# Compressed branch of a sparse attention kernel: four heads' probabilities turned by one transpose into a diagonal of blocks, values held four times

## The chip, the cores and the metric

One core of one Trainium2 chip runs the whole program. The metric is the device time of one execution in microseconds (us), the median of the runs shown. Engines are called as in the profile: PE (TensorE matmul), PEld (TensorE weight load, which overlaps PE), DVE (VectorE), ACT (ScalarE), POOL (GpSimd), SP (SyncE, which issues the DMAs).

## The reference, cut to what matters

The program is one transformer layer on 512 tokens of width 1024, all in float32: a gated feed-forward block, a mixer with two attention groups, a second feed-forward block, a last norm. One attention group (eight query heads in two key groups of four, head size 64) has three branches: a compressed one (31 block summaries as keys and values), a selected one and a windowed one, added with gates. The change touches the compressed branch alone:

```python
kc = compress_blocks(kc_raw, ...)        # 31 compressed keys per key group
vc = compress_blocks(vc_raw, ...)        # 31 compressed values per key group
s = jnp.einsum('btgrd,bcgd->bgrtc', q, kc) * ATTN_SCALE
s = jnp.where(mask_c, s - slopes[:, :, None, None] * dist_c, NEG_INF)
p_cmp = jnp.where(mask_c, jax.nn.softmax(s, axis=-1), 0.0)
o_cmp = jnp.einsum('bgrtc,bcgd->btgrd', p_cmp, vc)
...
return g[..., 0:1] * o_cmp + g[..., 1:2] * o_slc + g[..., 2:3] * o_win
```

With 8 selection blocks and 16 to choose, the selected branch is ordinary causal attention. For each block of 128 queries and each key group, `p_cmp` is four heads of 128 x 32 (the 32nd column is padding).

## The kernel before, in words

Every float32 matmul operand is split into a high part (float32r, a cast on ACT) and a low part (the difference, a subtraction on DVE), and a product takes two or three matmuls of these parts.

The order of the program is: the first feed-forward block, the mixer, the second feed-forward block. In the mixer, eight stages of the sliding-window group (class `Swa`) come first and then the stages of the sparse group (class `Nsa`): for key groups g = 0, 1 and query blocks i = 0 to 3, one stage with br = 0 for i = 0 and two stages, br = 1 (selected) and br = 2 (windowed), for i > 0. The compressed branch is computed within br = 0 and br = 2, so eight times in all.

A stage has two halves. `scores` (L1042 to L1133) makes the scores of four heads on PE (lines 985, 986, and a bias matmul on 1062, 1065, 1077 or 1098) in PSUM tiles `sc`, of which there are three. DVE takes the maximum (L1058, L1078), ACT the exponential (L1059, L1084), then DVE (L1116, L1117, L1128) and for one head in four ACT (L1126) scale the probabilities. The compressed probabilities of the four heads lie beside one another in one tile `small` (128 queries x 4 heads x 32), scaled on L1132. `outputs` (L1135 to L1153) makes a list of blocks and hands it to `times_values` (L1016): for each block `transposed` (L991) turns the probabilities of four heads by four PE transposes (L994) into one PSUM tile `mm`, ACT casts them into the high part (L996), DVE takes the low part (L997), and two matmuls (L1031 with the high part, L1032 with the low part) add values times probabilities into one PSUM tile `pv` (64 rows of the values' high part, 64 of their low part). The transposes of a block are written ahead of the matmuls of the block before. After the last block `put_o` (L1000) takes `pv` out: ACT copies the low rows (L1002), DVE adds them (L1007, twice), ACT and DVE split the sum (L1013, L1014). There is only one buffer for `pv`, so the first L1031 of the next stage waits for L1007.

In the compressed block the four transposes have 32 columns of probabilities as their weights and the identity as moving operand; the results, 32 x 128 each, lie side by side in rows 0 to 31 of `mm`. L996 and L997 work on 32 x 512 and write rows 0 to 31 of a fixed tile `ct` (the profile calls it `u` like others), whose other rows were set to zero at the start, as those of the values' tile `CV` were (L809). So the two matmuls of this block multiply 128 rows of which 96 are zero. `CV` gets its values on L895 and L896, once, before the first stage that needs them.

While the stages run, projections and the output product of the mixer (L216 to L218, three matmuls a step) are put in between as filler work by `attend`, by shares written as numbers. The order of instructions on each engine is then set when the program is built, by a scheduler with its own estimates of durations; a small change can move many instructions. On the chip each engine takes its queue in that order.

Of the kernel before, what the change touches and what calls it, by code (L numbers as in the profile page):

```python
# [12 lines left out]
AF = mybir.ActivationFunctionType  # L13
ALU = mybir.AluOpType
AX = mybir.AxisListType

P = 128
# [29 lines left out]
def tile_hybrid(ctx, tc, xT, f1_wi, f1_wo, wm_t, wm_n, cw1, cw2, small, wm_oa, wm_ob, wm_oc, f2_wi, f2_wo, const, out):  # L47
    nc = tc.nc
    V, A, PE = nc.vector, nc.scalar, nc.tensor
# [4 lines left out]
    def f(ap):  # L54
        return ap.bitcast(F32)

    def ps(tag="mm"):
        return psp.tile([P, 512], F32, tag=tag, name=tag, bufs=NB[tag])
# [8 lines left out]
    def flat(dt=F32R):  # L67
        return sb.tile([P, 1024], dt, tag="u", name="u", bufs=NU)

    def unit(dt=F32R):  # L70
        return flat(dt).rearrange("p (a t) -> p a t", a=2)
# [4 lines left out]
    def tmp():  # L76
        return sb.tile([P, 512], F32, tag="tmp", name="tmp", bufs=NTMP)
# [16 lines left out]
    ident = sb.tile([P, P], F32, tag="ident", name="ident")  # L94
# [708 lines left out]

    CV = sb.tile([P, 2, 2, HD], F32R, tag="cv", name="cv")
    ct = unit()
    zero = ones.unsqueeze(1).to_broadcast([P, 4, P])
    A.activation(CV.rearrange("p g a d -> p (g a d)").rearrange("p (a t) -> p a t", t=P), zero[:, :2], AF.Copy, scale=0.0)  # L809
    for a in range(2):  # L810
        A.activation(ct[:, a, :].rearrange("p (a t) -> p a t", t=P), zero, AF.Copy, scale=0.0)

# [57 lines left out]
    def network_o(kv):  # L870
        hT, w2 = state["hT", kv]
        po = ps()
        if kv == 0:
            for c in range(2):
                PE.matmul(po[:HD, :62], w2[:, c, :], hT[:, c, :], start=c == 0, stop=c == 1)
            kc = tmp()
            V.memset(kc[:HD, :64], 0.0)
            V.tensor_copy(
                kc[:HD, :64].rearrange("p (g c) -> p g c", g=2)[:, :, :NCMP],
                po[:HD, :62].rearrange("p (g c) -> p g c", g=2),  # L880
            )
            for g in range(2):
                put_key(kc[:HD, g * 32 : g * 32 + 32], 0, KT[g][0][:, 512:544], KT[g][1][:, 512:544])
        else:
            vc = tmp()
            V.memset(vc[:32, :128], 0.0)
            for g in range(2):
                for c in range(2):
                    PE.matmul(
                        po[:NCMP, g * HD : (g + 1) * HD], hT[:, c, g * NCMP : (g + 1) * NCMP], w2[:, c, :],  # L890
                        start=c == 0, stop=c == 1,
                    )
            V.tensor_copy(vc[:NCMP, :128], po[:NCMP, :128])
            vcv = vc[:32, :128].rearrange("p (g d) -> p g d", g=2)
            A.copy(CV[:32, :, 0, :], vcv)  # L895
            V.tensor_tensor(CV[:32, :, 1, :], vcv, f(CV[:32, :, 0, :]), op=ALU.subtract)  # L896
        yield 0.6


# [4 lines left out]
    def put_key(src, g, k1, k2):  # L904

        own = slice(g * HD, (g + 1) * HD)
        oth = slice((1 - g) * HD, (2 - g) * HD)
        A.copy(k1[own], src)
        V.tensor_tensor(k2[own], src, f(k1[own]), op=ALU.subtract)
        nc.sync.dma_start(f(k1[oth]), f(k1[own]))  # L910
        nc.sync.dma_start(f(k2[oth]), f(k2[own]))

    def keys(b, kind):
        o = ps()
        yield from proj(b, o)
        if kind == "b":
            SK.extend([unit(), unit()])
        elif not KT:
            for _ in range(2):
                k12 = double(F32R)  # L920
                KT.append([k12[:, :1056], k12[:, 1056:]])
        kz = tmp()
        V.tensor_tensor(kz, o, state["bc"], op=ALU.mult)
        for g in range(2):
            rows = slice(g * HD, (g + 1) * HD)
            if kind == "b":
                put_key(kz[rows, :], g, SK[0][:, g, :], SK[1][:, g, :])
            else:
                c = 544 if kind == "w" else 0
                put_key(kz[rows, :], g, KT[g][0][:, c : c + 512], KT[g][1][:, c : c + 512])  # L930


    VT = []
# [54 lines left out]
    def small_t(n, name):  # L988
        return sb.tile([P, n], F32, tag="st" + name, name=name, bufs=3)

    def transposed(pl, rows, cols):  # L991
        pt = ps()
        for r in range(4):
            PE.transpose(pt[:rows, r * P : (r + 1) * P], pl[r][:, cols], ident)  # L994
        u = unit() if rows == P else ct
        A.copy(u[:rows, 0, :], pt[:rows, :])  # L996
        V.tensor_tensor(u[:rows, 1, :], pt[:rows, :], f(u[:rows, 0, :]), op=ALU.subtract)  # L997
        return u

    def put_o(pv, kb0, i):  # L1000
        low = tmp()
        A.copy(low[lo, :], pv[hi, :])  # L1002
        pvv = pv.rearrange("p (a two t) -> p a two t", a=2, two=2)
        lov = low.rearrange("p (a two t) -> p a two t", a=2, two=2)
        ob = tmp()[:, :256].rearrange("p (a t) -> p a t", a=2)
        for par in range(2):
            V.tensor_tensor(ob[par * HD : (par + 1) * HD], pvv[lo, :, par, :], lov[lo, :, par, :], op=ALU.add)  # L1007
        ts = slice(i * P, (i + 1) * P)
        for a in range(2):
            if OB[kb0 + a] is None:  # L1010
                OB[kb0 + a] = unit()
            u = OB[kb0 + a]
            A.copy(u[:, 0, ts], ob[:, a, :])  # L1013
            V.tensor_tensor(u[:, 1, ts], ob[:, a, :], f(u[:, 0, ts]), op=ALU.subtract)  # L1014

    def times_values(work, pv, first, last):  # L1016

        ahead = None
        for n in range(len(work) + 1):
            if n < len(work):  # L1020
                pl, cols, rows, v = work[n]
                cur = transposed(pl, rows, cols), rows, v
                if n == 0:
                    yield 0.44
            else:
                cur = None
            if ahead is not None:
                u, rows, v = ahead
                a = first and n == 1
                b = last and n == len(work)  # L1030
                PE.matmul(pv, v, u[:, 0, :], start=a, stop=False)  # L1031
                PE.matmul(pv, v, u[:, 1, :], start=False, stop=b)  # L1032
                yield 0.87 if n < len(work) else 0.43
            ahead = cur

    class Nsa:
# [98 lines left out]
        def outputs(self):  # L1135
            g, i, br = self.g, self.i, self.br
            if br != 2:
                state["pv"] = ps("pv")
            pv = state["pv"]

            def values_of(b, kb):
                return VT[b][:, kb, g].rearrange("p a d -> p (a d)")

            if br == 0:
                work = [(self.p, slice(b * P, (b + 1) * P), P, values_of(b, 0)) for b in range(2)]
            else:
                work = [(self.p, slice(kb * P, (kb + 1) * P), P, values_of(br - 1, kb)) for kb in range(i + 1)]
            if br != 1:
                cl = [self.c[:, r, :] for r in range(4)]
                work.append((cl, slice(0, 32), 32, CV[:, g].rearrange("p a d -> p (a d)")))  # L1150
            yield from times_values(work, pv, br != 2, br != 1)
            if br != 1:
                put_o(pv, g * 2, i)  # L1153

    class Swa:
# [41 lines left out]
        def outputs(self):  # L1197
            g, i, W, c0 = self.g, self.i, self.W, self.c0
            pv = ps("pv")
            work = [  # L1200
                (self.p, slice(n * P, (n + 1) * P), P, VT[2][:, c0 // P + n, g].rearrange("p a d -> p (a d)"))
                for n in range(W // P)
            ]
            yield from times_values(work, pv, True, True)
            put_o(pv, 4 + g * 2, i)
# [68 lines left out]
    kb, vals = keys(8, "b"), values()  # L1274
# [15 lines left out]
    piece("c1", compressed(1))  # L1290
    piece("kw", keys(3, "w"))
    piece("o0", network_o(0))
    piece("n1", network(1))
    piece("q4", queries(4))
    piece("q5", queries(5))
    piece("o1", network_o(1))
    piece("q6", queries(6))
    piece("q7", queries(7))
# [122 lines left out]
```

## Time and profile before

| | before |
|---|---|
| median of 3 runs | 972.81 us (972.71 to 972.96) |
| the profiled execution | 972.98 us, of which the span shown is 971.2 us |
| granted clock of TensorE | 0.998 |
| PE busy | 957.0 us (99% of the span) |
| DVE busy | 814.8 us (84%) |
| ACT busy | 633.0 us (65%) |

The profile is of one execution. Matmuls are pipelined, and the busy time of PE includes the end of each one under the start of the next, so 99% does not mean that no time is lost on PE. The distance between the starts of two matmuls is what one costs when PE is the bound. "Idle before" names the engine whose semaphore came last.

### The profile page before, as it was taken

Reading aid. Unit: us, or ns where it says so; the run is one execution under the profiler, and the core shown is the slowest. Engines: PE = TensorE matmul, PEld = TensorE weight load, DVE = VectorE, ACT = ScalarE, POOL = GpSimd, SP = SyncE. Lnnn points to the kernel's source line nnn. Section 1 sums busy time; section 2 is a strip of 40 time slices with the busy share of each in tenths; the row PEclk is TensorE's granted clock in tenths of the full one; section 3 lists DMA queues with packets and bytes.
Section 4 is the critical chain, followed back from the end, with each engine's and each line's share of the span. In section 5 each row is a group of like instructions: output and inputs, shape, how many; then the busy total and the mean of one; then the engine's idle time right before and its main releaser. Section 6 shows DMA issues by size and latency. Waiting matters only on the chain.

```text
span 971.2 us, 13622 instructions
## 1 busy us (share of the span) xinstructions
PE 957.0 (99%) x5008; PEld 809.6 (83%) x5008; DVE 814.8 (84%) x1442; ACT 633.0 (65%) x1273; POOL 3.2 (0%) x7
## 2 busy tenths in 40 slices
PE   9999999999999999999999999999999999999996
PEld 7888888888888889788777888888888888888886
DVE  6999889888798675788899899999987988879864
ACT  8786666575766545554777776768667666676654
POOL 0000000000000000000000000000000000000000
PEclk9999999999999999999999999999999999999999
DMA  8233414234125213123310112223331423312122
GB/s 318 63 130 122 142 44 141 80 116 142 44 76 184 100 45 109 44 80 103 131 44 16 73 44 71 93 77 114 124 141 44 140 77 120 136 48 95 49 64 86
DMA packets 36387, 93.98 MB, mean 97 GB/s; under 512 B 4449, under 2 KB 8929, under 8 KB 36321
## 3 DMA queue, kind: packets, MB, share of 16 engines
q1 hardware_dynamic: 35648, 92.82, 27.7%
q8 instruction: 39, 0.64, 0.3%
q10 hardware_dynamic: 672, 0.30, 0.1%
q14 instruction: 28, 0.22, 0.1%
HBM read 89.40 MB, written 2.10 MB: 94 GB/s over the span
## 4 chain that ended last, share of the span: by engine, by line
PE 90%; DVE 4%; ACT 4%; issue 1%; DMA 1%; SPq 0%; POOL 0%; DVEq 0%; ACTq 0%
PE mm L352 18%; PE mm L353 9%; PE sc L352 7%; PE mm L218 4%; PE mm L216 4%; PE mm L217 4%; PE sc L353 4%; PE pv L441 4%; PE pv L443 3%; PE sc L441 3%; PE sc L442 3%; PE pv L442 3%; PE sc L443 3%; PE mm L994 2%; PE pv L1031 2%; PE sc L985 1%
## 5 line engine op out<-in xcount | busy, mean ns | idle before, releaser
L352 PE MATMUL mm<-u 128*128 128x512 f32 x760 | 273.6, 396 | 0.2 <-ACT mm L625 0.2
L353 PE MATMUL mm<-u 128*128 128x256 f32 x760 | 211.2, 279 | 0.0
L352 PEld LDWEIGHTS mm<-u 128*128 128x128 f32 x760 | 142.5, 188 | 34.2 <-DVE tmp L643 0.8
L353 PEld LDWEIGHTS mm<-u 128*128 128x128 f32 x760 | 143.2, 188 | 6.1
L352 PE MATMUL sc<-u 128*128 128x512 f32 x304 | 110.7, 396 | 0.0
L216 PE MATMUL mm<-u 128*128 128x512 f32 x220 | 88.3, 402 | 0.0
L217 PE MATMUL mm<-u 128*128 128x512 f32 x220 | 86.7, 394 | 0.0
L218 PE MATMUL mm<-u 128*128 128x512 f32 x220 | 86.5, 393 | 0.0
L353 PE MATMUL sc<-u 128*128 128x256 f32 x304 | 84.9, 279 | 0.0
L352 PEld LDWEIGHTS sc<-u 128*128 128x128 f32 x304 | 57.1, 188 | 13.2
L405 DVE TENSOR_TENSOR u<-tmp,u 128x512 fp32r<-128x512 f32 (+1 forms) x96 | 60.6, 641 | 8.0 <-ACT u L404 8.0
L404 ACT CAST u<-tmp 128x512 fp32r<-128x512 f32 (+1 forms) x96 | 54.8, 585 | 18.6 <-PE sc L443 13.6
L617 ACT COPY tmp<-mm 128x256 f32<-128x256 f32 x76 | 28.4, 374 | 50.5 <-PE mm L353 50.5
L353 PEld LDWEIGHTS sc<-u 128*128 128x128 f32 x304 | 57.2, 188 | 3.0
L441 PE MATMUL pv<-u 128*128 128x512 f32 x144 | 57.3, 398 | 0.0
L441 PE MATMUL sc<-u 128*128 128x512 f32 x144 | 57.1, 397 | 0.0
L443 PE MATMUL pv<-u 128*128 128x512 f32 x144 | 56.9, 395 | 0.0
L442 PE MATMUL sc<-u 128*128 128x512 f32 x144 | 56.7, 394 | 0.0
L442 PE MATMUL pv<-u 128*128 128x512 f32 x144 | 56.6, 393 | 0.0
L443 PE MATMUL sc<-u 128*128 128x512 f32 x144 | 56.2, 390 | 0.0
L330 DVE TENSOR_TENSOR u<-t,u 128x1024 fp32r<-128x1024 f32 x38 | 46.5, 1222 | 4.9 <-ACT u L327 2.8
L218 PEld LDWEIGHTS mm<-u 128*128 128x128 f32 x220 | 41.3, 188 | 8.2
(266 smaller groups left out, 2267.1 us busy)
## 6 DMA issues: line engine op xcount, KB each, us to landing
t<-in_f_wi_dram SPq DMA_DIRECT2D x87, 512.0 KB, 4.4
tmp<-in_f_wo_dram SPq DMA_DIRECT2D x80, 256.0 KB, 4.7
t<-in_wm_t_dram SPq DMA_DIRECT2D x13, 512.0 KB, 4.0
t<-in_cw_dram SPq DMA_DIRECT2D x8, 512.0 KB, 4.4
h<-in_xT_dram SPq DMA_DIRECT2D x4, 512.0 KB, 6.9
tmp<-in_f_wo_dram SPq DMA_DIRECT2D x16, 128.0 KB, 4.4
t<-in_wm_oa_dram SPq DMA_DIRECT2D x4, 512.0 KB, 3.9
t<-in_wm_n_dram SPq DMA_DIRECT2D x4, 408.0 KB, 5.2
```

Source lines behind the costliest of these rows:

```text
L216: PE.matmul(o, wh[:, c], xs[k][:, 0, :], start=s0, stop=False)
L217: PE.matmul(o, wh[:, c], xs[k][:, 1, :], start=False, stop=False)
L218: PE.matmul(o, wl[:, c], xs[k][:, 0, :], start=False, stop=s1)
L330: V.tensor_tensor(wl, t[:, 0:1024], f(wh), op=ALU.subtract)
L352: PE.matmul(o, w[0][:, c], x[k], start=new, stop=False, skip_group_check=not first)
L353: PE.matmul(o[:, :256], w[1][:, c], x[k][:, 0], start=False, stop=k == 3, skip_group_check=not first)
L404: A.copy(u[:, 0, :n], raw[:, :n])
L405: V.tensor_tensor(u[:, 1, :n], raw[:, :n], f(u[:, 0, :n]), op=ALU.subtract)
L441: PE.matmul(o, wh[:, c], u[:, 0, :], start=False, stop=False, skip_group_check=True)
L442: PE.matmul(o, wh[:, c], u[:, 1, :], start=False, stop=False, skip_group_check=True)
L443: PE.matmul(o, wl[:, c], u[:, 0, :], start=False, stop=q == j1 - j0 - 1, skip_group_check=True)
L617: A.copy(z, o[:, t2])
```

## The change: what it does

The compressed probabilities of the four heads, 128 x (4 x 32), are turned by one PE transpose of 128 columns (new line 997) in place of four of 32. The result has head r in rows 32r to 32r+31, over the 128 queries. To multiply each head with the same values and still get the four heads side by side in 512 columns, the 128 x 512 tile `ct` takes head r in rows 32r to 32r+31 and columns 128r to 128r+127, a diagonal of blocks; all else in it stays zero from the start. That takes four casts on ACT (new line 1000, 32 x 128 each) in place of one of 32 x 512, and four subtractions on DVE (new line 1002) in place of one. The values `CV` are written to all four quarters of its rows: three more copies on ACT, once (new line 898). The zeroing of `CV` (L809) goes, since all its rows are now written. The two matmuls of the block keep their shapes. The argument `rows` disappears from the list of blocks.

```diff
-    A.activation(CV.rearrange("p g a d -> p (g a d)").rearrange("p (a t) -> p a t", t=P), zero[:, :2], AF.Copy, scale=0.0)
...
             A.copy(CV[:32, :, 0, :], vcv)
             V.tensor_tensor(CV[:32, :, 1, :], vcv, f(CV[:32, :, 0, :]), op=ALU.subtract)
+            for r in range(1, 4):
+                A.copy(CV[r * 32 : r * 32 + 32], f(CV[:32]))
...
-    def transposed(pl, rows, cols):
+    def transposed(pl, cols):
         pt = ps()
+        if cols is None:
+
+            PE.transpose(pt[:, :P], pl.rearrange("p r c -> p (r c)"), ident)
+            at = [(slice(r * 32, r * 32 + 32), slice(r * P, (r + 1) * P)) for r in range(4)]
+            for rows, c in at:
+                A.copy(ct[rows, 0, c], pt[rows, :P])
+            for rows, c in at:
+                V.tensor_tensor(ct[rows, 1, c], pt[rows, :P], f(ct[rows, 0, c]), op=ALU.subtract)
+            return ct
         for r in range(4):
-            PE.transpose(pt[:rows, r * P : (r + 1) * P], pl[r][:, cols], ident)
-        u = unit() if rows == P else ct
-        A.copy(u[:rows, 0, :], pt[:rows, :])
-        V.tensor_tensor(u[:rows, 1, :], pt[:rows, :], f(u[:rows, 0, :]), op=ALU.subtract)
+            PE.transpose(pt[:, r * P : (r + 1) * P], pl[r][:, cols], ident)
+        u = unit()
+        A.copy(u[:, 0, :], pt)
+        V.tensor_tensor(u[:, 1, :], pt, f(u[:, 0, :]), op=ALU.subtract)
         return u
...
             if br != 1:
-                cl = [self.c[:, r, :] for r in range(4)]
-                work.append((cl, slice(0, 32), 32, CV[:, g].rearrange("p a d -> p (a d)")))
+                work.append((self.c, None, CV[:, g].rearrange("p a d -> p (a d)")))
```

Since the scheduler orders the queues anew, the change also moves other instructions of the sparse stages. Lines behind the added ones have other numbers after the change: 985 and 986 become 987 and 988, the transposes of L994 line 1005, L996 and L997 lines 1007 and 1008, L1002 and L1007 lines 1013 and 1018, L1031 and L1032 lines 1042 and 1043, L1058 and L1059 lines 1069 and 1070, L1062 and L1065 lines 1073 and 1076, L1116, L1117, L1126 and L1128 lines 1127, 1128, 1137 and 1139.

On PE, the end of the second stage with a compressed block (g = 0, i = 1, br = 2), from the low-part matmul of its compressed block to the next stage's work. Before:

```order
L1031 MATMUL pv<-u,cv 128x512
L1032 MATMUL pv<-u,cv 128x512
L985 MATMUL sc<-t_3949,u 128x416
L986 MATMUL sc<-t_3949,u 128x416
L1065 MATMUL sc<-u 128x32
L1062 MATMUL sc<-u 128x384
L217 MATMUL mm<-u 128x512
L218 MATMUL mm<-u 128x512
L994 MATMUL mm<-ident,tmp 128x128 x12
L985 MATMUL sc<-t_3949,u 128x416
L986 MATMUL sc<-t_3949,u 128x416
```

After the change:

```order
L1005 MATMUL mm<-ident,tmp 128x128 x7
L1043 MATMUL pv<-u,cv 128x512
L1005 MATMUL mm<-ident,tmp 128x128 x5
L1042 MATMUL pv<-u 128x512
L1043 MATMUL pv<-u 128x512
L1042 MATMUL pv<-u 128x512
L216 MATMUL mm<-u 128x512
```

The low-part matmul of the compressed block now stands within the next stage's twelve transposes, and only five of them lie between it and the first matmul into the next stage's `pv`.

On DVE, the same place: the subtractions of the compressed block and what follows them. Before:

```order
L997 TENSOR_TENSOR u<-mm,u 32x512
L1116 TENSOR_TENSOR su<-su,ge 128x4
L1058 TENSOR_REDUCE nm<-sc 128x1
L1117 RECIPROCAL su<-su 128x4
L1058 TENSOR_REDUCE nm<-sc 128x1
L1128 TENSOR_SCALAR tmp<-tmp,su 128x384 x3
L1007 TENSOR_TENSOR tmp<-pv,tmp 64x256 x2
```

After the change:

```order
L1002 TENSOR_TENSOR u<-mm,u 32x128
L1127 TENSOR_TENSOR su<-su,ge 128x4
L1002 TENSOR_TENSOR u<-mm,u 32x128
L1128 RECIPROCAL su<-su 128x4
L1002 TENSOR_TENSOR u<-mm,u 32x128
L1139 TENSOR_SCALAR tmp<-tmp,su 128x384 x3
L1002 TENSOR_TENSOR u<-mm,u 32x128
L1069 TENSOR_REDUCE nm<-sc 128x1 x3
L1018 TENSOR_TENSOR tmp<-pv,tmp 64x256 x2
```

The last of the four subtractions now stands behind the scaling of the next stage's probabilities, and three reductions stand between it and the two additions that release `pv`.

## Rows read from the trace of the kernel before

**Rows 1.** The page: the span and the busy time of each engine.

```profile
span 971.2 us, 13622 instructions
PE 957.0 (99%) x5008; PEld 809.6 (83%) x5008; DVE 814.8 (84%) x1442; ACT 633.0 (65%) x1273; POOL 3.2 (0%) x7
```

**Rows 2.** Busy time in 476 to 602 us: length, PE, PEld, DVE, ACT, POOL (instructions); granted clock, DMA.

```profile
476.00:602.00 126.00, 123.69 (x677) 101.05 (x676) 115.32 (x289) 98.10 (x296) 0.00 (x0) 1.00 0.15 53
```

**Rows 3.** The chain of waits, 476 to 602 us: shares by line, pieces.

```profile
by line: PE mm L994 14.3%; PE pv L1031 9.9%; PE mm L218 9.7%; PE mm L216 9.7%; PE sc L985 9.6%; PE mm L217 9.6%; PE pv L1032 8.8%; PE sc L986 8.0%; PE sc L1062 6.2%; ACT tmp L1059 2.0%; ACT u L996 1.9%; DVE u L997 1.5%; ACT tmp L1002 1.0%; 
478.34 0.87 PE mm L994 x8
560.67 1.20 PE mm L994 x11
```

**Rows 4.** Groups of instructions, 476 to 602 us, shapes apart: busy us, mean ns, idle before.

```profile
L994 PE MATMUL mm<-ident,tmp 128*128 128x128 f32 x168 | 26.1, 274 | 0.4 <-ACT tmp L1126 0.2 <-DVE tmp L1128 0.2
L994 PE MATMUL mm<-ident,small 128*32 128x128 f32 x32 | 5.1, 272 | 0.0
L996 ACT CAST u<-mm 32x512 fp32r<-32x512 f32 x8 | 4.5, 565 | 0.0
L997 DVE TENSOR_TENSOR u<-mm,u 32x512 fp32r<-32x512 f32 x8 | 5.4, 669 | 0.0
L1014 DVE TENSOR_TENSOR u<-tmp,u 128x128 fp32r<-128x128 f32 x16 | 4.0, 286 | 0.2
L1013 ACT CAST u<-tmp 128x128 fp32r<-128x128 f32 x16 | 4.0, 298 | 1.9 <-DVE tmp L1007 1.9
L1058 DVE TENSOR_REDUCE nm<-sc 128x1 f32<-128x384 f32 x16 | 8.5, 544 | 0.2 <-PE sc L1062 0.2
L1058 DVE TENSOR_REDUCE nm<-sc 128x1 f32<-128x32 f32 x32 | 6.0, 187 | 3.0 <-ACT tmp L1084 1.0 <-ACT tmp L1059 0.9 <-PE sc L1065 0.7
```

**Rows 5.** Single lines: counts, durations in ns min/median/max, first and last start, forms.

```profile
L617 ACT COPY tmp<-mm x76: 357/375/391, 54.8 to 935.4; 128x256 f32<-128x256 f32 x76
L896 DVE TENSOR_TENSOR cv<-tmp,cv x1: 280/280/280, 477.7 to 477.7; 32x128 fp32r<-32x128 f32 x1
L895 ACT CAST cv<-tmp x1: 298/298/298, 476.9 to 476.9; 32x128 fp32r<-32x128 f32 x1
L809 ACT ACTIVATE cv<-ones x1: 399/399/399, 2.6 to 2.6; 128x256 fp32r<-128x256 f32 x1
```

**Rows 6.** Timeline 505 to 509 us, a stage's end: start, duration, engine, line, operation.

```profile
505.17 0.39 PE L1031 MATMUL pv<-u,cv 128*128 128x512 f32 x1
505.40 0.39 PE L1032 MATMUL pv<-u,cv 128*128 128x512 f32 x1
505.83 0.58 ACT L1002 COPY tmp<-pv 64x512 f32<-64x512 f32 x1 [1.49 <-PE pv L1032]
506.72 0.84 DVE L1007 TENSOR_TENSOR tmp<-pv,tmp 64x256 f32<-64x256 f32 x2
508.08 0.49 ACT L1013 CAST u<-tmp 128x128 fp32r<-128x128 f32 x2
508.40 0.49 DVE L1014 TENSOR_TENSOR u<-tmp,u 128x128 fp32r<-128x128 f32 x2
508.90 0.46 PE L985 MATMUL sc<-t,u 128*128 128x416 f32 x1 [0.69 <-ACT small L1059]
```

**Rows 7.** Timeline 490 us: the first use of the compressed values.

```profile
490.20 0.39 PE L1031 MATMUL pv<-u,cv 128*128 128x512 f32 x1
```

**Rows 8.** Timeline at the start: ACT's first work behind L809.

```profile
5.40 0.72 ACT L170 ACTIVATE u<-h,sm 128x512 fp32r<-128x512 f32 x1 [2.43 <-DMA sm<-in_small_dram]
```

**Rows 9.** Waits of PE and of its weight load, 476 to 602 us: total us, times, longest.

```profile
PE sc L985 <- ACT small L1059: 1.0, 2, 0.7
PE sc L985 <- ACT tmp L1059: 0.7, 1, 0.7
PEld pv L1031 <- ACT u L996: 2.4, 9, 0.3
```

More of the change, by code (lines that the diff above doesn't have):

```diff
@@ L1020, in times_values @@
             if n < len(work):
-                pl, cols, rows, v = work[n]
-                cur = transposed(pl, rows, cols), rows, v
+                pl, cols, v = work[n]
+                cur = transposed(pl, cols), v
                 if n == 0:
@@ L1027, in times_values @@
             if ahead is not None:
-                u, rows, v = ahead
+                u, v = ahead
                 a = first and n == 1
@@ L1144, in outputs @@
             if br == 0:
-                work = [(self.p, slice(b * P, (b + 1) * P), P, values_of(b, 0)) for b in range(2)]
+                work = [(self.p, slice(b * P, (b + 1) * P), values_of(b, 0)) for b in range(2)]
             else:
-                work = [(self.p, slice(kb * P, (kb + 1) * P), P, values_of(br - 1, kb)) for kb in range(i + 1)]
+                work = [(self.p, slice(kb * P, (kb + 1) * P), values_of(br - 1, kb)) for kb in range(i + 1)]
             if br != 1:
-                cl = [self.c[:, r, :] for r in range(4)]
-                work.append((cl, slice(0, 32), 32, CV[:, g].rearrange("p a d -> p (a d)")))
+                work.append((self.c, None, CV[:, g].rearrange("p a d -> p (a d)")))
             yield from times_values(work, pv, br != 2, br != 1)
@@ L1200, in outputs @@
             work = [
-                (self.p, slice(n * P, (n + 1) * P), P, VT[2][:, c0 // P + n, g].rearrange("p a d -> p (a d)"))
+                (self.p, slice(n * P, (n + 1) * P), VT[2][:, c0 // P + n, g].rearrange("p a d -> p (a d)"))
                 for n in range(W // P)
```

## The prediction

> **What bounds the kernel now.** Read the page's busy times first [rows 1]: PE stands at 99% of the span, DVE at 84%, ACT at 65%. That says where to look, not what a change is worth, because the ends of matmuls overlap the starts of the next. The change works only in the sparse stages, so the second view is busy time in the stretch from 476 us (where the compressed values are written) to 602 us (the last take-out) [rows 2]: PE 123.7 of 126.0 us, DVE 115.3, ACT 98.1. The reader is to see that DVE is free for 10.7 us here, 8% of the stretch, against 16% over the span, and ACT for 27.9. The granted clock is 1.00 throughout, PE's upper level, and nothing in the change makes PE idle for long, so the clock has no term below.
>
> Third is the chain of waits of the same stretch [rows 3]. The lines of PE that it names add up to 85.8%, and the largest single one is the transposes, 14.3%. DVE and ACT have 6.4% in the named lines. So PE is the bound in nearly all of the stretch, and what is taken off PE's queue should show, unless it comes off in front of a wait. PE's own waits in the stretch are short: the longest group is 1.0 us in two times [rows 9].
>
> **The change part by part.** *Transposes.* Eight blocks lose three transposes each, 24 in all. A transpose is listed at 272 ns [rows 4], but that is its whole length; eight in a row take 0.87 us on the chain and eleven 1.20 [rows 3], so one costs 0.109 us. The form with 32 columns of weights has the same 272 ns as the form with 128 (274) [rows 4], and there are 32 of it: 8 blocks by 4. The one that is left is of the 128 form and costs no more. Gain: 24 x 0.109 = **2.62 us**. [...]
>
> *DVE.* One subtraction of 32 x 512, 669 ns [rows 4], becomes four of 32 x 128. The same operation on 32 x 128 took 280 ns [rows 5], from SBUF; on 128 x 128 it takes 286 [rows 4]. So four cost at most 4 x 0.280 = 1.12 us. Two of L1014 in a row take 0.49 [rows 6], so the second begins 0.20 after the first, and four in a row would be 3 x 0.20 + 0.28 = 0.88. The extra work is between 0.21 and 0.45 us a block, 1.7 and **3.6 us** in eight. In the new order some stand in a row and some apart; I take the middle, 2.7.
>
> *ACT.* One cast of 32 x 512, 565 ns [rows 4], becomes four of 32 x 128. From SBUF such a cast took 298 [rows 5]; a copy of 128 x 256 from PSUM takes 375 [rows 5], and with (565 - 375) / 256 = 0.74 ns a column, 128 columns come to 280. Two of L1013 in a row take 0.49 [rows 6], the second 0.19 after the first. Four cost between 3 x 0.19 + 0.28 = 0.85 and 4 x 0.298 = 1.19 us; extra 0.29 to 0.63 a block, 2.3 to 5.0 in eight. All eight groups stand four in a row in the new order, so I take 2.3.
>
> *What of this reaches the end.* DVE has 10.7 us free and ACT 27.9 [rows 2], so the work fits, but both take their queues in order, and a delay in front of an exponential or a take-out passes to PE when PE waits there. The two engines are on the chain for 6.4% of it [rows 3]. At that share 2.7 + 2.3 us give **0.3 us**. The ends are 0 (all hidden) and 3.6 (all of DVE's work on the path).
>
> *The block's own chain.* Before, the last matmul waits for four transposes (0.27 + 3 x 0.109), the cast (0.565) and the subtraction (0.669): 1.83 us. After, it is 0.27 + 0.85 and, since each subtraction needs only its own cast, one more of 0.28: about 1.4. Between the ends, from all four subtractions behind the last cast (0.27 + 0.85 + 1.12 = 2.24, a loss of 0.4) to the 1.4, nothing is charged: the new order puts the next stage's transposes between the turned block and its last matmul.
>
> *The border of two stages.* Here the order moves something that the edit does not name. Before, L1032 of the second compressed block starts at 505.40, and the two additions that free `pv` end at 506.72 + 0.84 = 507.56 [rows 6], 2.16 us later. In that time PE had four score matmuls, two fillers and twelve transposes. After the change only five transposes stand between that matmul and the next stage's first write to `pv`. PE's own work is 0.23 (the distance of two starts, 505.17 and 505.40 [rows 6]) + 5 x 0.109 = 0.77, so PE would stand for 2.16 - 0.77 = 1.39 us. Behind the waiting L1042 are the rest of the stage's value matmuls, fillers and the next scores, so nothing on PE passes it. But in the order before PE stands at this border too: L985 waits 0.69 us for an exponential [rows 6], and a wait for `pv` gives ACT that time. Net **+0.7 us**. The ends: 0, if the new order's reductions and exponentials gain as much elsewhere; and 1.39 + 1.6 = 3.0, if the three reductions now ahead of the two additions are all of the 384 form (544 ns [rows 4]) and come on top; of the small form (187 ns) they would add 0.6. I take the value nearest to the row at 505 us.
>
> *The copies of the values* are three of 32 x 256 on ACT once, each below the 399 ns of a 128 x 256 [rows 5]: at most 1.2 us behind 476.9 [rows 5], used first at 490.20 [rows 7], 13 us later. Zero; without that cover, 1.2. *The zeroing that goes* (L809, 0.40 us at 2.6 [rows 5]) stood before ACT's first scaling of the input at 5.40, which waited 2.43 us for a DMA [rows 8]. Zero. No DMA is moved: SP's and POOL's queues are the same in both orders.
>
> *Sum.* -2.62 + 0.7 + 0.3 = -1.6 us. The profiled execution took 972.98 us (span 971.2 and 1.8 around it), 0.17 above the median, so 971.4 by its own time and **971.2 us** against the median of 972.81. That is 0.17% faster. About 0.2%, or 1.95 us, is what a measurement of this kernel can tell from no change, so the likeliest case lies just inside.
>
> **The rivals.** *All of it (970.2 us).* PE is the bound everywhere, the border costs nothing net, and 2.62 us come off. For it: 123.7 of 126.0 busy and 85.8% of the chain in PE's named lines. Against it: five transposes over a take-out of 2.16 us.
>
> *DVE takes it back (972.6 to 974.5 us).* With 2.62 us less of stretch and up to 3.6 more of work, DVE would be busy 118.9 of 123.4 us, 96%. An engine in such a state, whose queue holds the maxima, the scaling, the low parts and the take-out, has no room to catch up; then its extra 1.7 to 3.6 us all reach the end: -2.62 + 0.7 + 1.7 = -0.2, and with 3.6, +1.7. Against it: DVE is on the chain for 1.5% in its one named line. [...]
>
> *Slower: the single `pv` (975.7 us).* The wait at the border of stages becomes the rule. There are seven borders behind a compressed block; at 1.39 us each, four of them give 5.6 - 2.62 = +2.9 us. That is the point from which it decides: (1.95 + 2.62) / 1.39 = 3.3. For it: one buffer, and the last subtraction now stands behind the next stage's scaling, which holds back L1043 and so the take-out. Against it: in the new order only one border is this short; at the others I count at least about 1.9 us of PE work at 0.23 a matmul of 512 and 0.109 a transpose.
>
> *It does not do what it says (972.8 us or a little more).* The removed transposes stood in front of waits for a cast, and PE now waits where it worked. For it: ACT's casts wait for transposes, so the two are close. Against it: the weight loads of L1031 wait for casts 2.4 us in nine times, at most 0.3 each, and PE itself has no such wait in its list [rows 9].
>
> **How the numbers follow.** The forecast (gain of 2.62 partly given back, some 970.5 to 972.4) gets 0.40, the full gain 0.25, DVE 0.18, the single `pv` 0.09, no effect 0.08. Faster by over 0.2% (under 970.86) is nearly all of the full gain, 0.22, and the lower part of the forecast, 0.10: 0.32. Slower (over 974.76) is the single `pv` and the top of DVE's case: 0.11. The rest, 0.57, lies within 0.2%. The range goes from 969.7 (the full gain, with most of the 0.69 us wait gone too) to 973.9 (most of DVE's case); left out are the single `pv`, the top of DVE and the tail below, together below 0.2.
>
> **What would show it.** Right: 8 transposes of the compressed form on PE in place of 32; four casts near 0.28 and four subtractions near 0.28 us a block; DVE above 94% of a stretch that is 1 to 2 us shorter; a wait of PE for DVE's additions of 1 us or more in front of L1042 at the second border. Wrong: that wait missing while the time is near 970 (the full gain); PE's waits for exponentials or maxima longer by 3 us in sum (DVE); waits for `pv` at four borders or more.

## The result and the profile after: 0.8% slower

The changed kernel takes 980.94 us (median of five, 979.83 to 981.25) against 972.85 (972.71 to 972.96) beside it: a ratio of 1.0079 with an interval of 1.0068 to 1.0091, **8.1 us more**. The prediction said 971.2, in 969.7 to 973.9. The profiled execution took 979.83 us.

First, where it lies. Two lines of the line view bracket the sparse stages: L889, a matmul just ahead of them, and L204, whose last instances stand behind them. Columns: count, durations in ns (min/median/max), first and last start. Before:

```profile
L889 PE MATMUL mm<-tmp,small x8: 219/219/243, 474.8 to 475.2; 128*31 128x64 f32 x8
L204 PE MATMUL pv<-ident,rcol x24: 270/275/376, 28.1 to 627.3; 128*128 128x128 f32 x24
```

After:

```profile
L889 PE MATMUL mm<-tmp,small x8: 219/219/243, 474.9 to 475.3; 128*31 128x64 f32 x8
L204 PE MATMUL pv<-ident,rcol x24: 270/275/376, 28.1 to 633.9; 128*128 128x128 f32 x24
```

From the first L889 to the last L204 it was 627.3 - 474.8 = 152.5 us, and is 633.9 - 474.9 = 159.0. So 6.5 of the 6.8 us that the two spans differ by came in here, and nothing ahead of 474 us. (The profiled execution is the shortest of after's five, so it shows less than the 8.1 of the medians.) I call this distance the *stages* below; it is free of the shift with which a whole execution can start later (the first L889 starts between 474.6 and 475.9 us in the runs below).

The page of after (span; busy us, share, instructions), then its busy time in the stretch of [rows 2], and in one of 6 us more, by about what the same work now takes longer (length, PE, PEld, DVE, ACT, POOL; granted clock, DMA):

```profile
span 978.0 us, 13615 instructions
PE 960.5 (98%) x4984; PEld 807.5 (83%) x4984; DVE 820.1 (84%) x1466; ACT 637.3 (65%) x1299; POOL 3.4 (0%) x7
```

```profile
476.00:602.00 126.00, 120.39 (x623) 93.62 (x622) 114.13 (x302) 97.29 (x313) 0.00 (x0) 1.00 0.13 49
476.00:608.00 132.00, 126.39 (x651) 98.28 (x650) 119.64 (x311) 102.22 (x322) 0.00 (x0) 1.00 0.14 50
```

PE still shows 98% and the clock 1.00. But in the same 126 us PE was busy for 120.4 us where it was for 123.7 [rows 2], and DVE (114.1 against 115.3) and ACT (97.3 against 98.1) were busy no longer either. The work on DVE and ACT has grown all the same: up to 608 us, near the end of the same work, DVE has 119.6 us and ACT 102.2, some 4 us more each, spread over 132 us. All three engines stand more: they wait for one another. The chain of waits from 476 to 602 us shows it (shares by line, then a piece: start us, us, what):

```profile
by line: PE mm L1005 7.4%; DVE nm L1069 7.1%; PE pv L1043 6.5%; PE sc L987 6.1%; PE mm L217 5.5%; PE mm L216 5.4%; PE pv L1042 5.2%; PE mm L218 5.1%; DVE u L1008 4.8%; PE sc L988 4.8%; ACT tmp L1070 4.2%; PE sc L1073 4.0%; ACT u L1007 3.7%;
509.19 1.49 DVE nm L1069 x3
```

DVE and ACT have 7.1 + 4.8 + 4.2 + 3.7 = 19.8% in the named lines, against 6.4% [rows 3]. The groups of instructions that the change made (busy us, mean ns, idle before):

```profile
L997 PE MATMUL mm<-ident,small 128*128 128x128 f32 x8 | 2.2, 279 | 0.0
L1000 ACT CAST u<-mm 32x128 fp32r<-32x128 f32 x32 | 8.2, 255 | 0.4
L1002 DVE TENSOR_TENSOR u<-mm,u 32x128 fp32r<-32x128 f32 x32 | 9.1, 283 | 0.5
L898 ACT CAST cv<-cv 32x256 fp32r<-32x256 f32 x3 | 1.2, 404 | 0.0
```

The counts are as forecast: 8 transposes for 32 [rows 4], each still near 0.28 us long, and casts and subtractions of 255 and 283 ns, at the estimate of 0.28. So the single durations were right, and the loss is in none of them alone. Waits of PE and of its weight load after the change, 476 to 602 us (total us, times, longest):

```profile
PE pv L1042 <- ACT u L1007: 2.1, 4, 1.4
PE sc L987 <- ACT tmp L1070: 1.2, 2, 1.0
PEld pv L1042 <- ACT u L1007: 4.4, 9, 1.6
PEld pv L1043 <- DVE u L1008: 4.4, 11, 0.7
```

Before, the same weight load waited 2.4 us in nine times, at most 0.3 [rows 9]; now it waits 4.4, at most 1.6. The weight load of the low part, L1043, waits another 4.4 us, and had no such row before.

### The profile page after: what moved, and what is told of

It reads as the page before. It is cut to its first block, busy times and chain, and to the rows that moved or that the text cites. A ratio compares the mean times of both kernels' runs of the same rounds, so it can differ in the third digit from the quotient of the medians.

```text
span 978.0 us, 13615 instructions
## 1 busy us (share of the span) xinstructions
PE 960.5 (98%) x4984; PEld 807.5 (83%) x4984; DVE 820.1 (84%) x1466; ACT 637.3 (65%) x1299; POOL 3.4 (0%) x7
## 4 chain that ended last, share of the span: by engine, by line
PE 85%; DVE 7%; ACT 5%; issue 1%; DMA 1%; SPq 0%; POOL 0%; DVEq 0%; ACTq 0%
PE mm L352 18%; PE mm L353 9%; PE sc L352 7%; PE mm L218 4%; PE sc L353 4%; PE mm L217 4%; PE mm L216 4%; PE pv L441 3%; PE pv L443 3%; PE sc L441 3%; PE sc L442 3%; PE pv L442 3%; PE sc L443 3%; PE mm L850 1%; PE mm L1005 1%; PE pv L1043 1%
## 5 line engine op out<-in xcount | busy, mean ns | idle before, releaser
L218 PE MATMUL mm<-u 128*128 128x512 f32 x220 | 86.4, 393 | 0.0
L218 PEld LDWEIGHTS mm<-u 128*128 128x128 f32 x220 | 41.3, 188 | 8.5
```

The costliest lines, as they stand in the source:

```text
L218: PE.matmul(o, wl[:, c], xs[k][:, 0, :], start=False, stop=s1)
```

## The experiments

Two theories stood at first. O: the order that the scheduler found anew costs the time. W: the many small casts and subtractions fill ACT and DVE. To part them, some kernels hold PE, DVE and ACT, over the sparse stages, to a written order (a chain of dependencies without a semaphore between neighbours of one queue, the numbers read from another kernel's program). In short form:

```diff
+    for told in ORDER:
+        seq = [by_name["I-%d" % n] for n in numbers(told)]
+        for a, b in zip(seq, seq[1:]):
+            tc.add_manual_dep(b, a.name, NOSYNC, reason="order")
```

All times in one table; "more" is against the runs of the kernel before beside it on the same chip (medians of 972.74 to 973.07), the interval is of the ratio, and "stages" is the distance of above in the profiled run. In e5, e6, e7 and e10 the output lacks part of the sum, as said for each; their time alone is of use.

| run | what | us | more | ratio, interval | stages |
|---|---|---|---|---|---|
| before | | 972.8 | | | 152.5 |
| after | the change | 980.94 | +8.1 | 1.0079 [1.0068, 1.0091] | 159.0 |
| e1 | the change, order of before | 979.15 | +6.1 | 1.0062 [1.0049, 1.0075] | 158.0 |
| e2 | before's work, order of after | 978.52 | +5.5 | 1.0056 [1.0043, 1.0068] | 157.4 |
| e3 | before, cast and subtraction in four, own order | 973.35 | +0.3 | 1.0003 [0.9994, 1.0012] | 152.7 |
| e4 | as e3, order free | 976.74 | +3.7 | 1.0037 [1.0024, 1.0051] | 157.2 |
| e5 | e1, all on partitions 0 to 31 | 974.21 | +1.3 | 1.0013 [1.0004, 1.0022] | 153.7 |
| e6 | e1 without the CV copies | 977.81 | +4.9 | 1.0049 [1.0032, 1.0066] | 157.1 |
| e7 | e3, output on four quarters | 977.02 | +4.1 | 1.0042 [1.0027, 1.0057] | 156.6 |
| e8 | diagonal in the values, eight matmuls | 975.30 | +2.4 | 1.0024 [1.0015, 1.0033] | 154.8 |
| e9 | pairs of heads, order of before | 972.74 | -0.3 | 0.9997 [0.9988, 1.0006] | 151.8 |
| e10 | after, all on partitions 0 to 31 | 977.90 | +4.8 | 1.0052 [1.0039, 1.0066] | 156.7 |
| e11 | as e9, order free | 970.40 | -2.7 | 0.9974 [0.9965, 0.9984] | 149.5 |
| e12 | after, border filled | 981.80 | +9.1 | 1.0089 [1.0072, 1.0106] | 161.0 |

**e1, e2: the order.** e1 is the changed kernel with an ORDER that repeats before's (the one transpose at the place of the last of four, the four casts at the place of the one, the copies behind L104's cast); e2 is the kernel before with after's ORDER.

> The changed work (one transpose a block, four casts, four subtractions, three copies of the values), with PE, DVE and ACT held to the order of the kernel before by edges that order the issue alone. Theory O (the new order of the queues costs the time; the edit itself gives what its transposes are worth): 970.2 to 971.5 us, PE's waits for value matmuls as before. Theory W (the small operations fill DVE and ACT, whatever the order): 979 to 982 us, near the changed kernel.

> The work of the kernel before (four transposes, one cast, one subtraction a block) in the order that the scheduler chose for the changed kernel; the cast stands where the first of the four casts stood, the subtraction where the last of the four subtractions stood. Theory O: 980 to 984 us, the loss of the changed kernel and the 2.6 us of transposes. Theory W: 972 to 975 us.

e1 lies where W had it, e2 between the two theories. Each costs most of the loss by itself, and 6.1 + 5.5 is more than 8.1, so they overlap. Neither theory had this.

**e3, e4: the small operations.** The change for the compressed block alone, where `at` is the four blocks of 128 columns:

```diff
-        A.copy(u[:rows, 0, :], pt[:rows, :])
-        V.tensor_tensor(u[:rows, 1, :], pt[:rows, :], f(u[:rows, 0, :]), op=ALU.subtract)
+        for c in at:
+            A.copy(ct[:rows, 0, c], pt[:rows, c])
+        for c in at:
+            V.tensor_tensor(ct[:rows, 1, c], pt[:rows, c], f(ct[:rows, 0, c]), op=ALU.subtract)
```

> The kernel before, its order held, with only the cast and the subtraction of a compressed block each split in four (32 x 128, by columns); the transposes stay four. Theory O: 972.8 to 974.5 us, at most what DVE's extra 1.7 to 3.6 us can cost. Theory W: 980 to 984 us.

> The same split in four with four transposes, but with the order left to the scheduler. It puts the border of the second and third stage as in the changed kernel (seven transposes, the low-part matmul, five transposes, the next stage's first value matmul). Theory O: 978 to 984 us, because the split alone already draws the new order. Theory W: as the split in the old order, within 1 us.

W falls as it stood: the same number of operations of the same size cost 0.3 us when the order holds, and the interval takes in none. With the order free the split alone costs 3.4 us more than that (e4, between the two theories). Then what had e1 that e3 had not? The timelines of the two show one block's four casts and four subtractions (start, duration of the group, count). e3:

```profile
542.03 0.72 ACT L998 CAST u<-mm 32x128 fp32r<-32x128 f32 x4
544.91 0.87 DVE L1000 TENSOR_TENSOR u<-mm,u 32x128 fp32r<-32x128 f32 x4
```

e1:

```profile
545.47 1.10 ACT L1000 CAST u<-mm 32x128 fp32r<-32x128 f32 x4
548.35 1.18 DVE L1002 TENSOR_TENSOR u<-mm,u 32x128 fp32r<-32x128 f32 x4
```

Four casts take 0.72 us and 1.10. With the 255 ns that one lasts in after, a cast of e3 starts (0.72 - 0.255) / 3 = 0.16 us after the one before, one of e1 0.28, when that has ended (0.26 in e1's groups of 1.04 us at 490.40 and 505.57). For the subtractions, with 283 ns for one, it is 0.20 and 0.30. What differs is that e1's four lie on partitions 0, 32, 64 and 96 in turn. Theory Q follows from this, and e5 to e7 test it both ways.

**e5, e7, e6: quarters and copies.**

```diff
 e5 (on e1)
-            at = [(slice(r * 32, r * 32 + 32), slice(r * P, (r + 1) * P)) for r in range(4)]
+            at = [(slice(0, 32), slice(r * P, (r + 1) * P)) for r in range(4)]
 e7 (on e3)
-                A.copy(ct[:rows, 0, c], pt[:rows, c])
+                A.copy(ct[q, 0, c], pt[:rows, c])
-                V.tensor_tensor(ct[:rows, 1, c], pt[:rows, c], f(ct[:rows, 0, c]), op=ALU.subtract)
+                V.tensor_tensor(ct[q, 1, c], pt[:rows, c], f(ct[q, 0, c]), op=ALU.subtract)
 e6 (on e1)
-            for r in range(1, 4):
-                A.copy(CV[r * 32 : r * 32 + 32], f(CV[:32]))
```

> The edit in the order of before, as in e1, but the four casts and four subtractions of a compressed block all read and write partitions 0 to 31 (the four blocks of columns as before); one transpose, three CV copies and the matmuls stay. This leaves out three of the four diagonal blocks. Theory Q (quarters): in the trace of e1 the casts start 0.268 us apart and the subtractions 0.298 us, in e3, where all lie on partitions 0 to 31, 0.157 and 0.198, with nearly the same duration of one; so a block holds ScalarE some 0.44 us and VectorE some 0.40 us longer, and PE waits for it. By Q the spacing is that of e3 again and the time 974.0 (972.5 to 975.5): 979.15 less 4 to 5.5 us. Theory T (the single transpose and the fewer matmuls uncover the chain): the time stays at 978 to 979.5, whatever the spacing.

> The kernel before in its own order, split as in e3, with four transposes and without CV copies, but the output of the four casts and subtractions goes to partitions 0, 32, 64 and 96 in turn; the sums over heads 1 to 3 are left out by it. Theory Q: spacing 0.27 and 0.30 us as in e1, and 977.5 to 979 us, 4 to 5.5 us over e3. Theory T: 973.4 as e3.

> The edit in the order of before, as in e1, without the three CV copies and with the zeroing of CV put back; this leaves out the values of three heads. Theory V: the copies stood on ScalarE's queue from 479.00 to 480.24 us, ahead of the exps, and PE's first values matmul came 1.01 us later against before: the time is 978.1 (1.0 us under e1). If the copies are hidden: 979.1.

e5 against e1 takes **4.8 us** off (6.1 to 1.3; by the stages 4.3) with the same count, sizes, matmuls and order; e7 against e3 puts 3.8 on, a little under its forecast. e5's and e7's groups of four:

```profile
543.44 0.72 ACT L1000 CAST u<-mm 32x128 fp32r<-32x128 f32 x4
546.31 0.87 DVE L1002 TENSOR_TENSOR u<-mm,u 32x128 fp32r<-32x128 f32 x4
```

```profile
543.68 1.08 ACT L998 CAST u<-mm 32x128 fp32r<-32x128 f32 x4
546.55 1.16 DVE L1000 TENSOR_TENSOR u<-mm,u 32x128 fp32r<-32x128 f32 x4
```

Theory Q is shown: the spacing on either engine, and the time for the two together; how much of the 4.8 us is ScalarE's and how much VectorE's is open, since no run has the quarters on one engine alone. e7's casts, whose inputs all lie on partitions 0 to 31, take 1.08 us against e3's 0.72: a new quarter of the output alone does it. T falls: with one transpose in place of four e5 takes 974.2, where T had 978 to 979.5. The copies cost 6.1 - 4.9 = 1.2 us (e6). Where, e1's ACT and PE rows show:

```profile
479.00 1.24 ACT L898 CAST cv<-cv 32x256 fp32r<-32x256 f32 x3
480.25 0.37 ACT L1095 ACTIVATE tmp<-sc,nm 128x128 f32<-128x128 f32 x1
480.95 1.07 ACT L1007 CAST u<-mm 128x512 fp32r<-128x512 f32 x2
481.58 0.50 PE L1042 MATMUL pv<-u 128*128 128x512 f32 x1 [0.89 <-ACT u L1007]
```

The copies hold ACT for 1.24 us, behind them stand two exponentials and the cast L1007, and for that cast PE's first L1042 waits 0.89 us.

**e8, e9, e11: other forms.** If the diagonal is what costs, it can lie in the values, which are written once. e8 does it with four tiles of values and matmuls of 128 columns; e9 and e11 with pairs of heads:

```diff
 e9, e11 (on the change)
-            PE.transpose(pt[:, :P], pl.rearrange("p r c -> p (r c)"), ident)
+            for r in range(2):
+                PE.transpose(pt[:96, r * P : (r + 1) * P], flat_p[:, r * 32 : r * 32 + 96], ident)
+            u = sb.tile([P, 2, 256], F32R, tag="cd", name="cd", bufs=2)
+            A.copy(u[:96, 0], pt[:96, :256])
+            V.tensor_tensor(u[:96, 1], pt[:96, :256], f(u[:96, 0]), op=ALU.subtract)
...
+                    for t in range(2):
+                        for h in range(2):
+                            PE.matmul(pv[:, h * 256 : h * 256 + 256], v[h], u[:96, t], ...)
...
-            for r in range(1, 4):
-                A.copy(CV[r * 32 : r * 32 + 32], f(CV[:32]))
+            A.copy(CV[64:96, 1], f(CV[:32, 0]))
```

> The same sum in another form, in the order of before: one transpose; one cast and one subtraction of 128x128 without the diagonal; the diagonal lies in the values (four tiles, each with its 32 rows, zero elsewhere), so eight matmuls of 128 columns in place of two of 512 a block; the three copies of the values stand later on ScalarE, where it was idle for 1.2 us at 486. Theory Q: nothing on quarters but the copies; a cast takes some 0.30 instead of 0.565 us and a subtraction 0.28 instead of 0.669; PE: eight at some 0.109 us, as the transposes take, in place of two at 0.23, and three transposes fewer, so +0.08 a block and +0.7 in all; less waiting gives some of it back: 972.5 (971 to 974). Theory T: as e1, 978 to 980.

> A third form of the same sum, in the order of before: two transposes of 96 columns each (heads 0 to 2, heads 1 to 3), one cast and one subtraction of 96x256, the values in two tiles (rows 0 to 31, rows 64 to 95, zero elsewhere), four matmuls of 256 columns; one copy of the values, on ScalarE at 486 us. Nothing is written on a quarter but that copy. A block has two transposes fewer on PE (0.218 us less; four of 256 columns at 0.12 take what two of 512 at 0.23 took), and a cast and a subtraction of half the columns (0.40 or so instead of 0.565 us, 0.41 instead of 0.669). Theory B (balance: before, PE, ScalarE and VectorE are so near one another in these stages that one engine's saving alone ends in a wait, as the saving of PE in e5 did, and that a saving on all three counts): 971.3 (970.0 to 972.7), against 972.9 before. If the savings end in waits for other work: 972.9.

> The form of e9, with the order left to the scheduler, which sets it anew. Reordering cost 3.4 us in e4 over e3 and 5.5 in e2 over before; theory O: 975 (973.5 to 978), 2 to 6 us over e9. If only the quarters cost, and any order does: as e9, 971.3 to 972.9.

e8's matmuls were dearer than taken, four in a row:

```profile
546.58 0.64 PE L1043 MATMUL pv<-cd,cv 128*128 128x128 f32 x4
```

Two of them take 0.39 us (at 544.79), so the distance is (0.64 - 0.39) / 2 = 0.125, and PE has 8 x 0.125 - 2 x 0.23 - 0.33 = 0.21 us more a block, 1.7 in eight. It paid 2.4 in all although a block's cast and subtraction had shrunk to 128x128, a form that takes 0.30 and 0.29 us in before [rows 4]. So the work added to PE was not hidden; the 0.7 us beyond it no run explains. In e9 and e11 cast and subtraction fall to 0.37 and 0.41 us, and PE has two transposes less. e11's groups, then its stretch 476 to 602 us, then the chain by line:

```profile
L998 ACT CAST cd<-mm 96x256 fp32r<-96x256 f32 x8 | 2.9, 367 | 0.0
L999 DVE TENSOR_TENSOR cd<-mm,cd 96x256 fp32r<-96x256 f32 x8 | 3.3, 408 | 0.0
```

```profile
476.00:602.00 126.00, 124.34 (x690) 103.21 (x689) 115.90 (x295) 98.28 (x299) 0.00 (x0) 1.00 0.15 54
```

```profile
by line: PE mm L1002 12.9%; PE mm L217 10.9%; PE mm L216 10.9%; PE mm L218 10.6%; PE sc L984 9.1%; PE pv L1044 8.8%; PE pv L1045 8.2%; PE sc L985 8.2%; PE sc L1075 6.2%; PE pv L1042 3.1%; PE mm L996 1.4%; ACT u L1004 1.3%; PE sc L1111 0.8%;
```

PE does 124.3 us of work in the stretch of 126, more than before's 123.7 [rows 2], DVE's lines are gone from the named chain and ACT has 1.3%. At 970.4 us **e11 is faster than both kernels**, 2.7 us under before and better than both its forecasts. In before's order the same form gains nothing that can be measured (e9): theory B misses there, and the gain comes only with the new order. Whether a saving on PE alone would have gained as well with its order free, no run tells. Theory O falls in its general form, since an order found anew can gain too.

**e10, e12: the new order.**

> The changed kernel in its own order (all three engines held to it), but the casts and subtractions on partitions 0 to 31 as in e5, which leaves out three of the four diagonal blocks. With e1, e5 and after this fills the square of order and quarters. If order and quarters add up: 980.9 less 4.9, 976.0. If the order is what costs by itself, as in e2 with the old work (5.5 us over before): 978 to 979.5.

e10 completes a square. With quarters, the order of after costs 8.1 - 6.1 = 2.0 us over that of before; without, 4.83 - 1.27 = 3.6; with the old work 5.5. In the profiled executions, of which after's is its shortest, the first of these is 159.0 - 158.0 = 1.0. The quarters cost 4.8 in before's order and 8.1 - 4.8 = 3.3 in after's. e10 lies between its two forecasts: order and quarters do not add up. That both feed the same waits, and part of each hides behind the other, would explain it but is not shown. e12 then moves six fillers in PE's ORDER ahead of the first L1042 at the second border:

> The changed kernel in its own order but for one place: at the border of the second and third sparse stage, where PE stood 1.59 us ahead of the first values matmul at 511.69, six filler matmuls that came 1 to 6 us later (four behind the third values matmul, two among the scores) stand ahead of it. Six at 0.23 are 1.4 us of PE work. If this border is 1.4 us of the loss for good (the step of the prediction, with its upper value): 979.5. If the stage is held by ScalarE's and VectorE's queues, and the fillers are missing where they stood: 980.9 as after.

After at this border:

```profile
509.21 0.50 PE L1043 MATMUL pv<-u,cv 128*128 128x512 f32 x1
509.55 0.71 PE L1005 MATMUL mm<-ident,tmp 128*128 128x128 f32 x5
509.87 0.58 ACT L1013 COPY tmp<-pv 64x512 f32<-64x512 f32 x1
510.47 1.07 ACT L1007 CAST u<-mm 128x512 fp32r<-128x512 f32 x2
509.19 1.49 DVE L1069 TENSOR_REDUCE nm<-sc 128x1 f32<-128x384 f32 x3
510.69 0.85 DVE L1018 TENSOR_TENSOR tmp<-pv,tmp 64x256 f32<-64x256 f32 x2
511.57 0.69 DVE L1008 TENSOR_TENSOR u<-mm,u 128x512 fp32r<-128x512 f32 x1
511.69 0.47 PE L1042 MATMUL pv<-u 128*128 128x512 f32 x1 [1.43 <-ACT u L1007]
```

e12:

```profile
509.45 0.71 PE L1005 MATMUL mm<-ident,tmp 128*128 128x128 f32 x5
512.30 0.72 PE L216 MATMUL mm<-u 128*128 128x512 f32 x1 [2.15 <-DVE u L1008]
512.83 0.63 PE L217 MATMUL mm<-u 128*128 128x512 f32 x1
514.96 0.63 PE L1042 MATMUL pv<-u 128*128 128x512 f32 x1
```

The wait that the prediction foresaw is there: behind the five transposes PE stands, and L1042 starts when DVE's two additions are through (510.69 + 0.85 = 511.54). The trace names the casts L1007, which end in the same moment (510.47 + 1.07). At the same place e10 waits 1.36 us and names the additions, and in e2, with before's work, PE has no matmul from 510 to 511 us, so the wait belongs to the order. But a filler in L1042's place does not start either, until 512.30, and there the trace names DVE's L1008, which reads the transposes' `mm` tiles. So this filler hangs on DVE as L1042 does, and there was nothing gained: 981.80 against 980.94, intervals overlapping. But behind this longer wait PE's granted clock also stood at 0.50, some 1.6 us of e12 by the estimate of the last section, which is more than the 1.4 us that were to be gained; so e12 does not settle what this border costs.

## Why the prediction was wrong

The prediction added -2.62 for the transposes, +0.7 for the border and +0.3 for what reaches the end of DVE's and ACT's work. Two of the three failed: the transposes gave back next to nothing, and of the work on DVE and ACT about 5 us reached the end, not 0.3. The copies, put at zero, cost 1 us or more, and the rest is the new order. The measured parts add up from before over e3 (+0.3), e5 (+1.0 more), e1 (+4.8) and after (+2.0) to 8.1. Step by step:

*Transposes, -2.62 us.* Count and 0.109 us each held. The gain did not: from e3 to e5 the transposes go and the copies come, and the time rises by 1.0, the stages from 152.7 to 153.7; the copies moved the first values matmul by just that (in e5 it starts 1.0 us later, counted from the first L889 in each). With 1.0 to 1.2 us for the copies, 24 transposes gave back 0 to 0.2 us (an estimate, as no run has the one transpose without quarters and copies). The timelines of e3 and e5 show how in one block (PE, start and duration). e3:

```profile
547.66 0.60 PE L994 MATMUL mm<-ident,small 128*32 128x128 f32 x4
548.01 0.48 PE L218 MATMUL mm<-u 128*128 128x512 f32 x1
548.33 0.39 PE L1038 MATMUL pv<-u 128*128 128x512 f32 x1
549.03 0.38 PE L985 MATMUL sc<-t,u 128*128 128x256 f32 x1
```

e5:

```profile
549.07 0.28 PE L997 MATMUL mm<-ident,small 128*128 128x128 f32 x1
549.10 0.48 PE L218 MATMUL mm<-u 128*128 128x512 f32 x1
549.55 0.47 PE L1042 MATMUL pv<-u 128*128 128x512 f32 x1
550.43 0.38 PE L987 MATMUL sc<-t,u 128*128 128x256 f32 x1 [0.18 <-ACT tmp L1070]
```

From the (first) transpose to L218 it is 0.35 us in e3 and 0.03 in e5; to the score matmul (L985, now L987) 1.37 and 1.36. What PE saved there, it waited for an exponential. This is the rival "it does not do what it says" as to the gain, and its 0.08 was too little. The step that failed: 85.8% of the chain in PE's lines [rows 3] was read as "what is taken off PE's queue should show, unless it comes off in front of a wait", and the gain was then taken whole. The share tells that more work on PE would show (e8), not that less would: where ACT and DVE follow within some tenths of a microsecond (0.18 in e5's last row), they end the next wait.

*DVE's and ACT's extra work, 2.7 + 2.3 us.* Mis-sized. In e1 four subtractions take 1.18 us, 0.51 more than 0.669, 4.1 us in eight, above the upper end of 3.6; four casts take 1.04 to 1.10, some 0.5 more, 4 us in eight, within its 2.3 to 5.0 but not the 2.3 that was taken. (In after only three of the eight groups of subtractions stand in a row; its 32 take 9.1 us in place of 5.4, 3.7 more.) The failed step is "the second begins 0.20 after the first", read from two instructions that write the same partitions (L1014). The other pair in the same group, L1007 at 506.72, took 0.84 us for two [rows 6], and those two write from partitions 0 and 64 on. After's L1018, the same pair, shows in the chain what that means, the second starting when the first has ended:

```profile
510.69 0.42 DVE tmp L1018
511.12 0.42 DVE tmp L1018
```

The evidence stood one row away. The runs show the same of the block's own pieces: from start to start 0.29 to 0.30 us on VectorE with the four on four quarters (e1, e7) against 0.20 on one (e3, e5), and on ScalarE 0.26 to 0.28 against 0.16.

*What of it reaches the end, +0.3 us by a share of 6.4%.* This is the step that cost most. From before to e3, ACT has 0.71 - 0.565 and DVE 0.87 - 0.669 us more a block, 2.8 us in eight, and 0.3 reach the end: 10%. From e5 to e1 it is another 0.33 to 0.38 and 0.31 a block, 5.1 to 5.5 us in eight, and 4.8 reach it: nine tenths (eight by the stages' 4.3). A share of the chain is not a rate: a block took up the first third of a microsecond of extra work, and most of what came on top reached the end. Nor was it the smallness of the pieces: with all on one quarter the split alone costs e3's 0.3 us. The rival in which DVE takes it back had the mechanism, but with DVE alone, and looked for it in a busy share above 94%; DVE shows 114.1 of 126, 91%. Its other sign, PE's waits for exponentials longer by 3 us, is missing too (1.4 us in sum against 1.7 [rows 9]).

*The copies of the values, zero.* They cost 1.0 to 1.2 us (e5, e6 in before's order). The words "used first at 490.20 [rows 7], 13 us later" looked at who reads them, not at who stands behind them on ACT. The prediction's own "without that cover, 1.2" was the value; each took 0.404 us, a little over the 0.399 that was to bound it.

*The border, +0.7.* The wait came, 1.43 us ahead of L1042, and only here: the other three of its kind share the remaining 0.7 of 2.1. Whether it costs anything for good is not shown, since e12's fillers met the same DVE and then a granted clock of 0.50. The rest of the new order's 2.0 us is spread over many short waits and **stays open**; e2 and e10 show that this order is worse for either work, not why.

*The block's own chain and L809, zero.* The first was not zero in its effect: it is the longer group of four, counted above. The second held: the first L889 starts at 474.8 and 474.9.

## What to carry to other kernels

Where three engines hand small tiles to one another and each is nearly full, price an edit by the queue: what stands behind the added instruction on its engine, and who waits for that. Here a saving on PE alone was worth next to nothing, an addition on DVE and ACT cost most of itself beyond the first tenths of a microsecond a block, and the one form that gained, the pairs, took from all three engines, though only in an order found anew for it. Before splitting an operation into pieces on different partitions, look in the trace for two neighbours that change partitions, and price the pieces end to end, as four casts took 0.72 us on one quarter (e3) and 1.10 on four (e1); and keep the order fixed in one run and free in another, since the scheduler's new order alone was worth between -2.3 (e11 against e9) and +5.5 us (e2) here.

## What had not been expected of the hardware

The four casts and the four subtractions of a block overlapped when all lay on partitions 0 to 31, and not when their outputs lay on partitions 0, 32, 64 and 96 in turn. A cast of 32x128 from PSUM on ScalarE followed the one before at 0.16 us, and at 0.26 to 0.28 when its output lay on another quarter; a subtraction on VectorE at 0.20 and at 0.29 to 0.30 (e3, e5 against e1, e7).

PE's granted clock fell behind the one long wait of e12. The profile's windows (length, busy times, granted clock, DMA):

```profile
511.00:512.00 1.00, 0.00 (x0) 0.00 (x0) 0.96 (x3) 1.00 (x4) 0.00 (x0) 1.00 0.00 0
513.00:514.00 1.00, 1.00 (x4) 0.81 (x3) 0.96 (x4) 1.00 (x7) 0.00 (x0) 0.50 0.06 16
516.00:517.00 1.00, 1.00 (x7) 0.93 (x6) 0.12 (x1) 0.00 (x0) 0.00 (x0) 1.00 0.00 0
```

PE had no matmul from 510.16 to 512.30, and from about 512.4 to 515.7 the granted clock was 0.50; a matmul of 512 columns took 0.63 us instead of 0.39. In after's profiled run the 1.43 us of waiting at the same place left the clock at 1.00. e4's profile shows the same fall, to 0.50 from 512 us on, behind a wait of 1.36, for about 3.4 us, so the length of the wait alone does not tell. Before's own trace has both values too: 1.00 in the stretch [rows 2], and 0.50 from 969 to 971 us, its last matmul having started at 963.48. The stages of e12 and e4 in the table hold some 1.6 us each that are the clock's, an estimate: in e12 eight matmuls stand at 0.43 instead of 0.23 us from start to start.
